# New prices and a looser dependency rule in the planner that writes a kernel's instruction order

## The chip, the cores and the metric

The kernel runs on one core of a Trainium2 chip. The metric is the device time of one execution in microseconds, the median over several runs. The core has five engines that work side by side, each with its own instruction queue that it goes through strictly in order: TensorE (PE in the profile, with its weight loads as PEld), VectorE (DVE), ScalarE (ACT), GpSimd (POOL) and SyncE (SP), which here only issues the transfers between memory and the core's SBUF. An instruction that needs another engine's result waits on a semaphore, and everything behind it on its engine waits with it.

## The reference

One inference step of a decoder with two layers and a width of 1024, for a prompt of 512 tokens and eight sample tokens that share all weights. In outline:

```python
h = x
for l in range(2):
    xn = rmsnorm(h, pre_norm_g[l])
    if l == 0:   # HGRN2: gated linear recurrence, 16 heads of 128
        q, fpre, i, z = split(xn @ w_in_a, 4)
        f = lb + (1 - lb) * sigmoid(fpre); k = 1 - f
        o, S = hgrn2_chunked(silu(q), log(f), k, i, S0)   # S_t = diag(f_t) S_{t-1} + k_t v_t^T
        mix = (rmsnorm(o, onorm_a) * silu(z)) @ w_out_a
    else:        # sliding window of 128, 32 query heads on 4 key/value heads, sinks, partial rotary
        k, v = split(rmsnorm(h, kv_norm_g) @ w_kv, 2)
        q, z = split(xn @ w_in_b, 2)
        mix = (window_attention(rope(q), rope(k), v, sinks) * silu(z)) @ w_out_b
    h = h + rmsnorm(mix, post_norm_g[l])
    h = h + (p[l] @ w_pe[l]) * sigmoid(h @ w_pg[l])
```

It returns h for all tokens, the final states of the recurrence and the new rows of keys and values. All arrays are 32-bit floats.

## The kernel before

Activations lie transposed, features on the 128 partitions and the 520 tokens along the free axis. A weight matrix is worked through in tiles of 128 output features; a tile takes up to 8 steps over the input features, and a step is six matmuls of 260 columns, because each 32-bit operand is split into a high and a low part (high x high, low x high, high x low, for two halves of the tokens). The weights come in loads of 512 KB into one of three buffers (`wr`); ScalarE copies the high part into `wh`, VectorE or GpSimd takes the difference into `wl` (`halves`, lines 649 to 659). TensorE sums a tile in a PSUM pair `pj`, and ScalarE or VectorE empties it. Beside this main stream run the chains of small steps: in layer A one chain a head (`hgrn` and `sample_a`), in layer B one a unit of attention heads (`unit_attn`). These use the four PSUM banks `ph`. The tiles `xs` and `og` hold the split inputs of the matmuls, `sb` the states of the sample tokens, `b` the small work tiles, `acc` the sums of squares for a norm.

A turn of a tile (`turn`, line 922) is done through memory: VectorE transposes blocks into `tmp`, one transfer writes them to `td`, and four transfers read them back, each into 32 partitions of the turned tile `xr`. In layer B, `query` (line 1266) swaps halves through `qd` in the same manner, with two writes and two reads.

The kernel has no fixed order of instructions. Every instruction is first entered into a plan (`Plan.enter`, line 187) with its level (MAIN, SIDE or FIRST), the engines that may run it, a price, and the earlier instructions that it depends on. `Plan.issue` (line 233) then plays the program through on model clocks, one for each engine, and writes the instructions out in the order in which the model starts them. That order is the program: on the chip nothing is reordered. What decides in it:

- `price` (line 142) gives each instruction's busy time, and whether it holds the port that VectorE and GpSimd share.
- `after` (line 241) adds a hand-over: `SAME` when maker and user are on the same engine, `LAT` for another engine, 0.1 for a transfer. `ready` (line 247) is the latest of these over an instruction's dependencies.
- `choose` (line 261) takes, on each engine, the instructions that could start first. On TensorE those that came ready less than `HAND` = 0.3 us ago go behind the others; on the three engines in `SHY` so do, in layer A, those that read a transfer landed less than `SAFE` = 1.5 us ago. Then the level decides, then the place in the program.
- A transfer starts when one of the `lanes` is free; its bytes go through one common `pipe`, and it lands some time behind that (lines 320 to 325). Loads that depend on nothing are held back while the pipe's backlog is over `BACKLOG`.
- A tile name taken from a fixed number of buffers has a maker, its first user. Every other instruction that touches the tile depends on the maker, whether or not the two touch the same bytes. The chip itself waits only for what overlaps.

The first loads, a warm-up of TensorE and six tiles of the embedding (`embed`) open the program; the masks `lmask` are made beside it on GpSimd and VectorE. Where a layer ends, the sums of squares go through a matmul with `ones`, a power on GpSimd (`rsr`) and a transposition into `R`, and then `residual` (line 777) makes the new `xs` step by step on VectorE and ScalarE, for the first matmuls of `gates` (line 798) with the weights `w_pg`. Tiles of the embedding fill TensorE meanwhile.

All instructions are recorded by one line of `enter`, 192, so the profile tells them apart by their tiles.

Of the kernel before, what the change touches and what calls it, by code (L numbers as in the profile page):

```python
# [53 lines left out]

SAME = {"tensor": -0.3, "vector": 0.05, "scalar": 0.1, "gpsimd": 0.02}
LAT = {"tensor": 0.28, "vector": 0.2, "scalar": 0.25, "gpsimd": 0.17}
HAND = 0.3
SAFE = 1.5
SHY = ("tensor", "vector", "scalar")

BEGIN = {"tensor": 0.9, "vector": 0.8, "scalar": 2.0, "gpsimd": 0.7, "sync": 0.0}

IDLE, SLOW = 3.4, 6.8
LATE = 1.5

RUNS = ((64, 4.0), (128, 2.0), (256, 1.4), (512, 1.15))
BACKLOG, CALM = 1.5, 40.0
# [27 lines left out]
class Plan:  # L95
# [46 lines left out]
    def price(self, engine, op, aps, a, k):  # L142
# [3 lines left out]
        if engine == "sync":  # L146
            run = min(self.run(x) for x in aps)
            return aps[0].nbytes() / 3.3e5 * next((f for n, f in RUNS if run <= n), 1.0), False
        if engine == "tensor":
            n, m = int(np.prod(aps[0].shape[1:])), int(np.prod(aps[1].shape[1:]))  # L150
            if op == "transpose":
                return 0.109, False
            if aps[1].dtype == F32:
                return 2 * max(0.025, 0.109 * m / P, n / 1200 + 0.003), False
            if aps[1].dtype == F32R:
                return max(0.109, 0.000453 * n + 0.002), False
            return n / 2400 + 0.003, False
# [7 lines left out]
        if engine == "scalar":  # L165

            t = 0.06 + 0.00086 * size * (3.2 if a[0].ap[-1][0] == NB else 1) + part
            if "accum_out" in k:
                t += 0.26 if AF.Exp in a else 0.19
            return t, False  # L170
# [3 lines left out]
        if op == "copy_predicated":  # L174
            return 0.09 + 0.0011 * size, False
        if op == "tensor_reduce":
# [10 lines left out]
    def enter(self, on, name, a, k):  # L187
# [6 lines left out]
        if any(x.tensor.name.startswith("tw") for x in ins[1:]):  # L194
            op.late = LATE
        self.ops.append(op)
        for x in ins:
            t = x.tensor.name
# [4 lines left out]
            if kept and t not in self.left:  # L203
                tag, bufs = self.homes.get(t, (t, 1))
                if tag not in self.slots:
                    self.slots[tag] = Slots(tag, bufs)
                self.slots[tag].order.append(t)
                op.news.append((tag, t))
                self.maker[t] = op
            elif kept:  # L210
                op.deps.add(self.maker[t])
            if t not in op.tiles and kept:
                op.tiles.add(t)
                self.left[t] = self.left.get(t, 0) + 1
        for x in outs:
# [8 lines left out]
            self.writes.setdefault(t, []).append((r, op))  # L224
        op.deps.discard(op)
        op.load = op.dma and not op.deps
        for d in op.deps:
# [5 lines left out]
    def issue(self):  # L233
        clock = dict(BEGIN)
        wait = {e: [] for e in clock}
        homes = {t: tag for tag, s in self.slots.items() for t in s.order}
        given, pipe, lanes, low, port, slow = set(), 0.0, [0.0] * 8, 0, 0.0, 0.0
        best = dict.fromkeys(clock)
        stale = set(clock)

        def after(d, e):

            if d.dma:
                return d.end + 0.1
            return d.end + (SAME if d.engine == e else LAT)[d.engine]

        def ready(op, e):
            return max((after(d, e) for d in op.deps), default=0.0)

# [11 lines left out]
        def choose(e):  # L261
# [13 lines left out]
            safe = SAFE if t > CALM and low < self.second else 0.0  # L275
            fresh = lambda op: any(d.dma and d.end + safe > t for d in op.deps)
            able.sort(
# [25 lines left out]
        while todo:  # L303
# [16 lines left out]
            if op.dma:  # L320
                t = max(t, lanes[0])
                clock[e] = t + 0.45
                pipe = max(pipe, t + 1.4) + cost
                op.end = pipe + 1.6 + op.late
                lanes = lanes[1:] + [op.end]
# [1515 lines left out]
```

## Time and profile before

| what | value |
|---|---|
| median of 3 runs | 1069.0 us (1067.67 to 1069.65) |
| the profiled execution | 1068.61 us |
| span of the program in it | 1066.8 us |
| granted TensorE clock, mean | 0.999 |
| TensorE busy | 1057.2 us, 8828 matmuls |
| VectorE, ScalarE, GpSimd busy | 904.7, 681.8, 114.0 us |
| moved by transfers | 178.99 MB, mean 168 GB/s |

The span runs from the first instruction to the last end in one profiled execution; the execution's own time is 1.8 us longer, for what lies around the program. A row of the stretches gives, for 27 us, the busy time of each engine with its number of instructions, the granted clock, the busy share of the transfer engines and the GB/s. A row in order of time gives start, length, engine, operation, tiles and shapes, a count where several of a kind were merged, and in brackets how long the engine sat idle before it and for whom. Groups give busy time, the mean of one in ns, and the idle time before. Layer A ends and layer B begins at some 570 to 620 us, and layer B ends from about 1000 us.

### The profile page before, as it was taken

To read this page: it belongs to the slowest core of one execution; us is meant where nothing else is said; L and a number is where in the kernel's file an instruction comes from. 1 tells how busy PE (TensorE), PEld (TensorE's weight loads), DVE (VectorE), ACT (ScalarE), POOL (GpSimd) and SP (SyncE) were. 2 spreads that over 40 slices of the span, in tenths; PEclk is the share of its full clock that TensorE was granted. 3 is DMA by queue.
4 is the path that set the end of the run, shared out by engine and by line. 5 is a ranking of instruction groups with operands and counts; after the bars stand their busy time and mean duration, and the time that the engine had idled before them with its cause. 6 is when DMAs were issued, how large, how long until landed. Compare 5 with 4: busy or idle time off the path is not lost.

```text
span 1066.8 us, 23981 instructions
## 1 busy us (share of the span) xinstructions
PE 1057.2 (99%) x8828; PEld 1051.2 (99%) x8828; DVE 904.7 (85%) x1963; ACT 681.8 (64%) x1829; POOL 114.0 (11%) x198
## 2 busy tenths in 40 slices
PE   9999999999999999999999999999999999999998
PEld 8999999999999999999999999999999999999998
DVE  8899788875787958788889999699999998999894
ACT  7877676655767637776636565477667664675542
POOL 1111121101111112111111000000100000002000
PEclk9999999999999999999999999999999999999999
DMA  9556586665646646576663454544433545423432
GB/s 314 183 190 183 143 247 195 191 195 156 213 155 206 193 130 224 177 210 191 190 223 142 159 190 142 170 121 136 124 101 115 164 155 186 154 82 124 156 100 81
DMA packets 147069, 178.99 MB, mean 168 GB/s; under 512 B 76932, under 2 KB 99660, under 8 KB 146952
## 3 DMA queue, kind: packets, MB, share of 16 engines
q1 hardware_dynamic: 146952, 177.46, 52.7%
q8 instruction: 70, 1.15, 0.4%
q14 instruction: 47, 0.39, 0.1%
HBM read 137.04 MB, written 34.86 MB: 161 GB/s over the span
## 4 chain that ended last, share of the span: by engine, by line
PE 91%; ACT 4%; DVE 3%; issue 1%; DMA 0%; POOL 0%; DVEq 0%; POOLq 0%
PE pj L192 71%; PE ph L192 21%; ACT g L192 1%; ACT wh L192 1%; DVE wl L192 1%; DVE x L192 0%; DMA wr<-in_w_pg 0%; ACT tmp L192 0%; ACT sb L192 0%; ACT b L192 0%; DVE acc L192 0%; ACT og L192 0%; DVE xr L192 0%; DVE tmp L192 0%; DVE g L192 0%
## 5 line engine op out<-in xcount | busy, mean ns | idle before, releaser
L192 PE MATMUL pj<-xs,wh 128*128 128x260 f32 (+2 forms) x3264 | 554.7, 285 | 1.6 <-ACT xs L192 1.3
L192 PEld LDWEIGHTS pj<-xs,wh 128*128 128x128 f32 x3264 | 457.7, 189 | 3.2 <-ACT xs L192 2.3
L192 PE MATMUL pj<-xs,wl 128*128 128x260 f32 (+2 forms) x1632 | 340.5, 285 | 0.0
L192 PEld LDWEIGHTS pj<-xs,wl 128*128 128x128 f32 x1632 | 255.1, 188 | 0.2
L192 ACT CAST wh<-wr 128x512 fp32r<-128x512 f32 x287 | 176.2, 619 | 111.1 <-PE pj L192 100.5
L192 DVE TENSOR_TENSOR wl<-wr,wh 128x512 fp32r<-128x512 f32 x275 | 187.6, 685 | 48.6 <-ACT wh L192 47.4
L192 PE MATMUL pj<-og,wh 128*128 128x260 f32 x1056 | 182.4, 285 | 0.3 <-ACT og L192 0.3
L192 PEld LDWEIGHTS pj<-og,wh 128*128 128x128 f32 x1056 | 149.5, 188 | 0.9 <-ACT og L192 0.5
L192 PE MATMUL pj<-og,wl 128*128 128x260 f32 x512 | 106.3, 284 | 0.1
L192 PEld LDWEIGHTS pj<-og,wl 128*128 128x128 f32 x512 | 79.9, 188 | 0.3 <-DVE wl L192 0.3
L192 ACT ACTIVATE sb<-sb,g 128x128 f32<-128x128 f32 x128 | 64.7, 556 | 2.4 <-DVE sb L192 2.4
L192 ACT ACTIVATE sb<-sb,nv 128x128 f32<-128x128 f32 x128 | 63.1, 555 | 0.3
L192 ACT COPY b<-ph 128x256 f32<-128x256 f32 (+1 forms) x80 | 27.8, 350 | 47.0 <-PE ph L192 46.5
L192 ACT ACTIVATE b<-b,an 128x129 f32<-128x129 f32 x128 | 50.6, 398 | 4.5 <-DVE an L192 4.4
L192 ACT ACTIVATE tmp<-pj 128x520 f32<-128x520 f32 (+2 forms) x48 | 24.5, 527 | 43.3 <-PE pj L192 43.2
L192 PE MATMUL ph<-xs,b 128*128 128x256 f32 (+1 forms) x360 | 50.5, 283 | 0.0
L192 DVE COPY_PREDICATED xr<-lmask,ph 128x256 f32<-128x256 int32 x96 | 46.8, 487 | 3.8 <-PE ph L192 3.4
L192 PE MATMUL ph<-xr,b 128*128 128x128 f32 x320 | 49.0, 275 | 0.3 <-ACT b L192 0.3
L192 DVE TENSOR_TENSOR x<-x,pj 128x520 f32<-128x520 f32 (+2 forms) x64 | 39.5, 621 | 10.8 <-PE pj L192 10.2
L192 DVE TENSOR_TENSOR g<-g,b 128x256 f32<-128x256 f32 x96 | 40.5, 422 | 9.3 <-ACT b L192 6.1
L192 DVE TENSOR_TENSOR xr<-xr,b 128x256 f32<-128x256 f32 x96 | 41.0, 427 | 8.6 <-PE ph L192 6.4
L192 PEld LDWEIGHTS ph<-xs,b 128*128 128x128 f32 x360 | 46.3, 188 | 0.1
(222 smaller groups left out, 1737.8 us busy)
## 6 DMA issues: line engine op xcount, KB each, us to landing
wr<-in_w_in_a SPq DMA_DIRECT2D x64, 512.0 KB, 4.5
sb<-sd SPq DMA_DIRECT2D x32, 512.0 KB, 4.5
wr<-in_w_in_b SPq DMA_DIRECT2D x32, 512.0 KB, 4.0
td<-tmp SPq DMA_DIRECT2D x45, 256.0 KB, 3.2
xr<-td SPq DMA_DIRECT2D x180, 64.0 KB, 3.2
sb<-in_state SPq DMA_DIRECT2D x16, 512.0 KB, 5.4
out_st_s<-sb SPq DMA_DIRECT2D x16, 512.0 KB, 3.0
wr<-in_w_out_a SPq DMA_DIRECT2D x16, 512.0 KB, 4.8
```

What stands on the lines that cost most here:

```text
L192: op = Op(len(self.ops), self.level, on, [lambda c=c: c(*a, **k) for c in calls], [self.price(e, name, ins, a, k) for e in on], on[0] == " ...
```

## The change

Four things change, all of them in the planner:

1. The hand-overs `SAME` and `LAT` get other values, most of them lower.
2. The model of transfers: SyncE's clock begins at 0.45 us; 16 transfers may be under way instead of 8; a transfer enters the pipe 1.2 us after its issue instead of 1.4 and lands 1.8 us (`LAND`) behind its bytes instead of 1.6; the rates are given outright, by the shortest contiguous run, and are lower for short runs.
3. The prices of instructions: on ScalarE by whether the input is in PSUM, with a term for a stride of eight elements and one for each operand that holds one value a partition (in place of the one for sums); on VectorE for predicated copies and for transposes; on TensorE in the last digits.
4. The dependency on a tile's maker is kept for the order (the maker is still issued first) but is left out of `ready` and of the question whether a transfer is fresh, unless the two overlap in the data.

```diff
-SAME = {"tensor": -0.3, "vector": 0.05, "scalar": 0.1, "gpsimd": 0.02}
-LAT = {"tensor": 0.28, "vector": 0.2, "scalar": 0.25, "gpsimd": 0.17}
+SAME = {"tensor": -0.28, "vector": 0.034, "scalar": 0.06, "gpsimd": 0.02}
+LAT = {"tensor": 0.31, "vector": 0.12, "scalar": 0.14, "gpsimd": 0.12}
 HAND = 0.3
+LAND = 1.8
-BEGIN = {"tensor": 0.9, "vector": 0.8, "scalar": 2.0, "gpsimd": 0.7, "sync": 0.0}
+BEGIN = {"tensor": 0.9, "vector": 0.8, "scalar": 2.0, "gpsimd": 0.7, "sync": 0.45}
-RUNS = ((64, 4.0), (128, 2.0), (256, 1.4), (512, 1.15))
+RATES = ((64, 5.0e4), (128, 1.0e5), (256, 1.4e5), (512, 2.3e5), (1e9, 3.0e5))
...
             run = min(self.run(x) for x in aps)
-            return aps[0].nbytes() / 3.3e5 * next((f for n, f in RUNS if run <= n), 1.0), False
+            return aps[0].nbytes() / next(r for n, r in RATES if run <= n), False
...
             if op == "transpose":
-                return 0.109, False
+                return 0.111, False
             if aps[1].dtype == F32:
-                return 2 * max(0.025, 0.109 * m / P, n / 1200 + 0.003), False
+                return 2 * max(0.025, 0.111 * m / P, n / 1200 + 0.003), False
             if aps[1].dtype == F32R:
-                return max(0.109, 0.000453 * n + 0.002), False
+                return max(0.111, 0.0004427 * n + 0.00475), False
...
         if engine == "scalar":
-            t = 0.06 + 0.00086 * size * (3.2 if a[0].ap[-1][0] == NB else 1) + part
-            if "accum_out" in k:
-                t += 0.26 if AF.Exp in a else 0.19
+            t = (0.06 if aps[1].space == PSUM else 0.085) + 0.00085 * size + part
+            if a[0].ap[-1][0] == NB and size > 64:
+                t += 0.0012 * size
+            near = sum(int(np.prod(x.shape[1:])) == 1 < size for x in aps[2:])
+            t += (0.1 if size > 64 else 0.15) * near
             return t, False
...
         if op == "copy_predicated":
-            return 0.09 + 0.0011 * size, False
+            return (0.07 + 0.00104 * size if apart else 0.1 + 0.00115 * size), False
+        if op in ("transpose", "stream_shuffle"):
+            return 0.1 + 0.00104 * size, False
...
+        makers = set()
         for x in ins:
...
             elif kept:
-                op.deps.add(self.maker[t])
+                makers.add(self.maker[t])
...
         op.deps.discard(op)
+        op.soft = makers - op.deps - {op}
+        op.deps |= op.soft
         op.load = op.dma and not op.deps
...
-        given, pipe, lanes, low, port, slow = set(), 0.0, [0.0] * 8, 0, 0.0, 0.0
+        given, pipe, lanes, low, port, slow = set(), 0.0, [0.0] * 16, 0, 0.0, 0.0
...
         def ready(op, e):
-            return max((after(d, e) for d in op.deps), default=0.0)
+            return max((after(d, e) for d in op.deps if d not in op.soft), default=0.0)
...
-            fresh = lambda op: any(d.dma and d.end + safe > t for d in op.deps)
+            fresh = lambda op: any(d.dma and d.end + safe > t for d in op.deps if d not in op.soft)
...
-                pipe = max(pipe, t + 1.4) + cost
-                op.end = pipe + 1.6 + op.late
+                pipe = max(pipe, t + 1.2) + cost
+                op.end = pipe + LAND + op.late
```

The computation, the tiles, the buffers and the number of instructions are the same; only their order, and which of VectorE and GpSimd takes a step that both may take, can differ.

## The prediction

> **What bounds the kernel now.** I read the page first, then the busy time by stretches, then what TensorE (PE) waited for, then the order of time around each of its waits. The page says that TensorE is the bound:
>
> ```profile
> span 1066.8 us, 23981 instructions
> PE 1057.2 (99%) x8828; PEld 1051.2 (99%) x8828; DVE 904.7 (85%) x1963; ACT 681.8 (64%) x1829; POOL 114.0 (11%) x198
> ```
>
> The change removes no matmul, so what it can win is TensorE's idle time, and that sits in few places. Stretches of 27 us, columns as in the page (busy PE first); left out are stretches that read 27.00, and one of them is shown:
>
> ```profile
> 0.00:27.00 27.00, 24.89 (x189) 23.09 (x190) 23.86 (x59) 19.44 (x38) 4.54 (x18) 1.00 0.90 313
> 27.00:54.00 27.00, 26.89 (x224) 26.66 (x224) 23.13 (x42) 22.93 (x47) 4.90 (x10) 1.00 0.54 179
> 54.00:81.00 27.00, 26.68 (x224) 26.44 (x223) 25.59 (x50) 20.13 (x48) 3.32 (x8) 1.00 0.59 199
> 81.00:108.00 27.00, 26.79 (x229) 26.59 (x229) 24.68 (x61) 20.62 (x57) 3.40 (x8) 1.00 0.62 185
> 135.00:162.00 27.00, 27.00 (x231) 27.00 (x230) 24.09 (x59) 19.79 (x49) 5.68 (x10) 1.00 0.83 259
> 567.00:594.00 27.00, 25.56 (x205) 24.50 (x204) 26.26 (x66) 17.36 (x44) 3.19 (x3) 1.00 0.54 186
> 594.00:621.00 27.00, 26.91 (x225) 26.71 (x224) 26.97 (x70) 17.94 (x49) 0.00 (x0) 1.00 0.43 153
> 675.00:702.00 27.00, 26.80 (x224) 26.54 (x224) 18.84 (x38) 17.29 (x50) 1.18 (x1) 1.00 0.46 142
> 999.00:1026.00 27.00, 25.87 (x215) 25.37 (x214) 26.32 (x69) 18.11 (x43) 2.53 (x2) 1.00 0.33 115
> 1053.00:1080.00 27.00, 9.78 (x81) 9.57 (x79) 3.37 (x9) 1.46 (x4) 0.00 (x0) 0.94 0.07 25
> ```
>
> Idle are 2.11 us in the first stretch, 0.11 + 0.32 + 0.21 to 108 us, 1.44 + 0.09 where layer A ends, 0.20 at 675, 1.13 where layer B ends, and 13.8 - 9.78 = 4.02 in the last. The last is the tail behind the final matmul (an activation, two VectorE steps, a store), which no order shortens. What TensorE waited for, with total, times and longest:
>
> ```profile
> PE pj L192 <- ACT xs L192: 1.3, 2, 0.8
> PE ph L192 <- DVE far L192: 1.1, 1, 1.1
> PE pj L192 <- DVE g L192: 0.9, 2, 0.6
> PE ph L192 <- ACT b L192: 0.5, 2, 0.3
> PE ph L192 <- DVE acc L192: 0.5, 1, 0.5
> PE ph L192 <- POOL rsr L192: 0.4, 1, 0.4
> PE pj L192 <- ACT og L192: 0.3, 1, 0.3
> PE ph L192 <- DVE ad L192: 0.2, 1, 0.2
> ```
>
> The 1.1 us on far is the launch. The other ten waits make 4.1 us. An idle gap shows less than it costs, because matmuls overlap:
>
> ```profile
> 652.55 33.96 PE pj L192 x283
> L192 PE MATMUL pj<-xs,wh 128*128 128x260 f32 x2944 | 496.7, 285 | 0.1
> ```
>
> One matmul each 33.96 / 283 = 0.120 us, while one lasts 0.285: a gap hides 0.285 - 0.120 = 0.165 us before it is seen. After a gap a pair takes 0.48 us (the matmul row at 5.24 us, below) where 0.285 + 0.120 = 0.405 is usual: 0.08 more. I take 0.25 us on top of each gap. Ten waits cost 4.1 + 2.5 = 6.6 us. The gaps too short for the list (about 4.5 us of idle inside, less 4.1) add 0.4, and with some five of them another 1.3. So 8.3 us is the ceiling of any better order.
>
> **The change part by part.** All of it acts through the order that the planner writes; no engine works faster.
>
> *Prices of TensorE.* A 260-column matmul goes from 0.000453 x 260 + 0.002 = 0.1198 to 0.0004427 x 260 + 0.00475 = 0.1199 us, beside the measured 0.120. Cost nothing; a wrong price here would move every stretch, and it is right in both.
>
> *The first loads (a loss).* SyncE now begins at 0.45 instead of 0, and a load lands at 1.2 + size / 3.0e5 + 1.8. The first 128 KB piece was planned for 1.4 + 0.40 + 1.6 = 3.4 us and is now planned for 0.45 + 1.2 + 0.44 + 1.8 = 3.9. The trace has it earlier than both:
>
> ```profile
> 2.92 0.41 ACT L192 CAST wh<-tmp 128x256 fp32r<-128x256 f32 x1 [0.60 <-DMA tmp<-in_w_pe]
> 2.99 1.33 DVE L192 TENSOR_SCALAR lmask<-lmask 128x256 int32<-128x256 int32 x4 [0.32 <-POOL lmask L192]
> 5.24 0.48 PE L192 MATMUL pj<-g,wh 128*128 128x260 f32 x2 [0.63 <-DVE g L192]
> ```
>
> Mask steps, which nothing needs yet, already fill VectorE ahead of what TensorE waits for, and a later planned landing invites one more (1.33 / 4 = 0.33 us). Bounds 0 and 0.5 (the shift); I take +0.3, nearest to one mask step.
>
> *Prices of ScalarE (a gain).* At 57.34 TensorE waits for a copy that ScalarE reached late:
>
> ```profile
> 55.41 0.54 ACT L192 ACTIVATE sb<-sb,g 128x128 f32<-128x128 f32 x1
> 55.84 0.71 ACT L192 ACTIVATE g<-g,ones 128x512 f32<-128x512 f32 x1
> 56.46 0.54 ACT L192 ACTIVATE sb<-sb,g 128x128 f32<-128x128 f32 x1
> 56.90 0.39 ACT L192 COPY b<-g 128x256 f32<-128x256 f32 x1
> 57.34 0.71 PE L192 MATMUL ph<-xr,b 128*128 128x128 f32 x4 [0.32 <-ACT b L192]
> ```
>
> From start to start the first three take 56.90 - 55.41 = 1.49 us. Old prices: 0.06 + 0.00086 x 128 x 3.2 = 0.41, 0.06 + 0.00086 x 512 = 0.50, 0.41, in all 1.32: 0.17 short. New: 0.085 + 0.109 + 0.154 + 0.1 = 0.45, 0.085 + 0.435 + 0.1 = 0.62, 0.45, in all 1.52: right. The two waits on ACT b cost 0.5 + 2 x 0.25 = 1.0, and the idle of 27 to 54 us, 0.11, with its 0.25 makes 0.4. Bounds: 0 (the copy has other reasons to be late) and 1.4. The prices are off just there, so I take -1.2. The wait on ACT og I leave as it is, since no row says what would fill it.
>
> *End of layer A, 567 to 594 us.* The idle 1.44 + 0.09 with some six gaps of 0.25 is 3.0 us.
>
> ```profile
> 572.75 0.41 DVE L192 TENSOR_TENSOR acc<-acc,tmp 128x256 f32<-128x256 f32 x1
> 573.45 1.46 POOL L192 TENSOR_TENSOR wl<-wr,wh 128x512 fp32r<-128x512 f32 x1 [17.61 <-ACT wh L192]
> 573.69 1.85 DVE L192 TENSOR_TENSOR acc<-acc,tmp 128x256 f32<-128x256 f32 x2
> 575.25 0.60 PE L192 MATMUL ph<-ones,acc 128*128 128x1 f32 x4 [0.50 <-DVE acc L192]
> 587.75 5.01 DMA wr<-in_w_pg
> 592.79 1.14 ACT L192 CAST b<-wr 128x512 fp32r<-128x512 f32 x2 [1.22 <-DMA wr<-in_w_pg]
> ```
>
> Three causes: first, two VectorE additions took 1.85 us while GpSimd worked, where one just before took 0.41; TensorE lost 0.50 + 0.25 = 0.75. Second, ScalarE sat 1.22 us before a weight piece whose load took 5.01 us; the casts of xs that TensorE wants stand behind it. The old price of that load is 1.4 + 1.59 + 1.6 + 0.1 = 4.69, the new 1.2 + 1.75 + 1.8 + 0.1 = 4.85: half of the 0.32 us that was missing. Third, VectorE is full (26.26 and 26.97 of 27 us), which no price changes. Bounds 0 and -2.25 (3.0 less the 0.75); I take -1.0, nearer to 0 because of the full VectorE.
>
> The Trainium skill, page SBUF — State Buffer, section SBUF: two separate sides, says that VectorE with two SBUF inputs and GpSimd take one shared pair of ports as an exclusive lock, and that the loser waits for the whole instruction. The 1.85 us beside the 1.46 agree. By that rule it is decided by which starts first on the chip, and the 0.75 us stay or fall by chance, and the sum is as it stands; were it a matter of prices alone, the sum would end 0.75 lower.
>
> *End of layer B and 675 us.* The idle 1.13 with two gaps of 0.25 is 1.63 us, and at 675 it is 0.20 + 0.25 = 0.45. The first has the same chain of norm and casts on a VectorE that is busy 26.32 of 27. Bounds 0 and -2.1; I take -0.7, a third, as above.
>
> *A tile's first user.* This acts on transfers above all. Four reads fill one turned tile; the later three were planned behind the landing of the first, though their rows are apart:
>
> ```profile
> xr<-td SPq DMA_DIRECT2D x180, 64.0 KB, 3.2
> 313.64 0.57 SPq L192 DMA_DIRECT2D xr<-td  x1
> 316.42 1.93 SPq L192 DMA_DIRECT2D xr<-td  x3
> ```
>
> The gap of 2.8 us is the planned landing. Now the four go out together and the tile is whole about 2 us sooner, 45 times. It wins nothing: between 108 and 567 us, where most of them are, TensorE reads 27.00, and before that no wait in the list is on a transfer. The short pieces of these reads are priced higher too (64 KB in runs of 128 bytes from 0.40 to 0.66 us), which holds weight loads back in the plan by up to 4 x 0.26 = 1.0 us a turn; sixteen transfers may be in flight instead of eight, which lets them go earlier. The cover of it all: a weight load behind three such issues leaves 1.9 us later (the row above), and three weight buffers last 3 x 48 x 0.120 = 17 us. If that cover were gone, each turn would cost up to 1.9 + 1.0 us.
>
> *VectorE's prices.* A predicated copy of 256 from PSUM goes from 0.37 to 0.34 us, a transpose gets 0.03 more. Cost nothing: a shift this small is under the 0.3 us by which TensorE waits a fresh step out. Without that it would be 0.03 a step.
>
> *Hand-overs.* ScalarE's falls from 0.25 to 0.14 us and VectorE's from 0.20 to 0.12. The copy at 56.90 ends at 57.29 and TensorE starts at 57.34: price and hand-over were 0.28 + 0.25 = 0.53, are 0.30 + 0.14 = 0.44, and measure 0.44. So 0.09 us of slack goes from each. Bounds 0 and +8.8 (the rival below); I take +0.0 because TensorE still ranks a step that came ready under 0.3 us ago behind all others.
>
> Sum: +0.3 - 1.2 - 1.0 - 0.7 = -2.6 us. The profiled execution took 1068.6 us, and 1066.0 follows; the median of the three runs is 0.4 higher, and on it I forecast **1066.4 us**. What a measurement can tell from no change is about 0.2%, 2.1 us.
>
> **The rivals.**
>
> *The waits only move (no change).* VectorE at 26.26, 26.97 and 26.32 of 27 us is the true limit at both ends of layers; then only the ScalarE term is won: -1.2 + 0.3 = -0.9, 1068.1 us. For it: these three rows. Against it: 5.01 us of a load planned at 4.69 is a fault of price.
>
> *The slack was needed (slower).* TensorE takes its steps in a fixed order, so one late hand-over stops all behind it.
>
> ```profile
> L192 ACT COPY b<-g 128x256 f32<-128x256 f32 x80 | 32.0, 401 | 8.8 <-DVE g L192 7.5 <-PE ph L192 1.0
> ```
>
> These 80 copies, and about 50 others of their kind in layer A, feed TensorE, and 2 of them stop it now. With 0.09 us less, a late one costs about 0.09 + 0.25 = 0.34. Above (2.6 + 2.1) / 0.34 = 14 late ones the kernel is slower; one in seven, 18, gives 6.1 - 2.6 = +3.5, 1072.5 us. Bound: one in five, 26, is 8.8 - 2.6 = +6.2. Against it stands the 27.00 of the stretches from 108 to 567 us, where even ScalarE prices that were short by 0.17 stopped nothing.
>
> *The rule of the first user does nothing.* If the chip itself held the later three reads until the first had landed, the new order would have SyncE wait there. SyncE would lose 2.8 us a turn, and the turned tiles would come no sooner; with the other terms as they are, 1066.4 again. The same time, so it shares the forecast's chance.
>
> **How the numbers follow.** Forecast 0.44, waits that only move 0.31, slack needed 0.25. Each case spreads: the forecast from two thirds of the 8.3 us ceiling (-5.5, 1063.5) to the edge at 1066.9, the second to 1071.1, the third from there up. The range 1063.5 to 1073.0 leaves one in ten at each side; the likeliest case alone is 1063.5 to 1066.9. Faster 0.44, same 0.31, slower 0.25.
>
> **What would show it.** Right: TensorE's busy time stays at 1057 and its idle inside falls from 4.5 us to about 3; no wait on ACT b before 108 us; the wait of ScalarE on the weight load at the end of layer A under 0.8 us; the first matmul on real data at 5.2 to 5.7 us; the four reads of a turn issued together. Wrong: new waits on copies (ACT b, ACT g) in stretches that read 27.00 now, which is the slower case; or the same idle at 567 and 999 us with VectorE still above 26, which is no change. Any idle stretch of several us where none was would make it wrong in a way that I do not foresee: a new order that leaves a buffer late.

## The result and the profile after

The changed kernel takes 1073.4 us (median of 5 runs, 1073.2 to 1074.7), the kernel before beside it 1068.5 (1067.7 to 1069.7). The ratio is 1.0050, with an interval of 1.0036 to 1.0063: slower by 4.9 us, where I had forecast 2.6 us less. The profiled execution took 1074.71 us, its span is 6.1 us longer than that of before. The page after:

```profile
span 1072.9 us, 23983 instructions
PE 1060.2 (99%) x8828; PEld 1053.7 (98%) x8828; DVE 906.2 (84%) x1968; ACT 680.8 (63%) x1829; POOL 116.4 (11%) x193
```

The matmuls are as many as before; 3.0 us of the 6.1 are in TensorE's busy time, which also grows when matmuls run slowly, and 3.1 in its idle time. The stretches after, columns as before:

```profile
0.00:27.00 27.00, 23.83 (x163) 21.93 (x164) 22.80 (x55) 18.93 (x37) 4.41 (x17) 1.00 0.91 308
135.00:162.00 27.00, 26.69 (x226) 26.49 (x225) 22.57 (x51) 17.73 (x48) 4.74 (x11) 1.00 0.49 143
567.00:594.00 27.00, 26.61 (x223) 26.28 (x222) 26.23 (x65) 18.83 (x45) 1.66 (x2) 1.00 0.53 166
675.00:702.00 27.00, 26.16 (x217) 25.77 (x216) 20.23 (x37) 17.92 (x57) 1.43 (x1) 1.00 0.45 140
702.00:729.00 27.00, 26.12 (x216) 25.67 (x215) 25.20 (x50) 16.78 (x48) 2.38 (x3) 1.00 0.38 112
783.00:810.00 27.00, 25.99 (x213) 25.37 (x213) 25.93 (x62) 17.17 (x63) 2.72 (x2) 1.00 0.37 101
999.00:1026.00 27.00, 25.89 (x216) 25.42 (x215) 25.50 (x63) 17.27 (x42) 2.26 (x2) 1.00 0.46 155
```

567 to 594 us is better by a whole microsecond, from 54 to 108 us, not shown, the idle time is gone. But 702 to 729 and 783 to 810 us, which read 27.00 before, have lost 0.9 and 1.0, 675 to 702 has 0.84 idle instead of 0.20, and the first stretch 3.17 instead of 2.11. What TensorE waited for after:

```profile
PE ph L197 <- DVE b L197: 1.7, 2, 0.9
PE pj L197 <- DVE g L197: 1.2, 1, 1.2
PE ph L197 <- DVE far L197: 1.1, 1, 1.1
PE ph L197 <- DVE g L197: 1.0, 1, 1.0
PE pj L197 <- ACT xs L197: 0.8, 2, 0.4
PE pj L197 <- DVE wl L197: 0.8, 1, 0.8
PE ph L197 <- POOL rsr L197: 0.7, 1, 0.7
PE ph L197 <- DVE xr L197: 0.3, 1, 0.3
```

The waits on ACT b, ACT og and DVE acc are gone. VectorE has taken their place, with few and long stops. To see where time was lost, busy or idle, I gave every matmul its usual pitch (0.120 us for 260 columns, 0.118 for 256, and so on; the sum is the same in every kernel here) and worked out from the matmuls' starts how much later than the kernel before each kernel had done the same work. I call this its lag. Single entries are good to some 0.4 us: so far do they move with another choice of the usual pitches.

```
where before is at  after  l_ties  l_table  l_four  s_a30  n_b071   (us later)
10                  2.31    0.87    2.10     0.12    0.89   0.46
30                  2.96    1.50    2.70     0.91    1.49   1.00
100                 1.77    0.27    1.55    -0.27   -0.50   0.49
160                 2.57    0.62    2.35     0.08   -0.18   0.71
520                 2.94    1.00    2.73     1.33    0.00   1.05
640                 0.93   -0.98    0.44    -0.99   -2.12   4.13
700                 1.76   -0.17    0.14    -0.83   -1.00   3.79
730                 3.11    0.13    1.43    -0.58    0.59   4.91
820                 5.19    1.34    3.61     0.28    1.18   4.68
1000                5.60    1.60    3.90     1.07    3.74   4.09
last matmul's end   5.49    1.45    3.85     1.00    3.69   4.11
behind it           0.61    0.61    0.61     0.37    0.01   0.00
```

The other columns belong to the experiments. After loses 3.0 us in the first 30, wins 1.2 up to 100, loses 0.8 near 145, wins 2.0 at the end of layer A, loses 4.3 between 640 and 820 and 0.6 behind the last matmul. Four things in the trace stand at the places of loss.

*The start.*

```profile
1.78 0.89 DVE L192 TENSOR_SCALAR lmask<-lmask 128x256 int32<-128x256 int32 x2 [0.77 <-POOL lmask L192]
2.24 3.01 DVE L197 TENSOR_SCALAR lmask<-lmask 128x256 int32<-128x256 int32 x9 [1.22 <-POOL lmask L197]
5.17 0.41 DVE L197 TENSOR_TENSOR wl<-tmp,wh 128x256 fp32r<-128x256 f32 x1
6.07 0.77 PE L197 MATMUL pj<-g,wh 128*128 128x260 f32 x2 [1.20 <-DVE g L197]
6.64 0.64 PE L197 MATMUL pj<-g,wl 128*128 128x260 f32 x2
```

The first row is of the kernel before, which had these two and the four at 2.99 us: nine mask steps instead of six stand ahead of the first difference of weights. TensorE begins on data at 6.07 instead of 5.24 us, and then two matmuls take 0.64 us where 0.40 is usual, a pitch of 0.215 instead of 0.120, until about 10 us. I call this half pitch. Of the five executions three took 1073.2 to 1073.4 us and two 1074.7, the profiled one among these; so the half pitch, some 1.5 us of the 3.0, is probably not in the median.

*VectorE beside GpSimd.* At two places a VectorE step takes over a microsecond more than its like, and TensorE stops behind it:

```profile
700.57 1.68 POOL L197 TENSOR_TENSOR g<-g,tmask 128x512 fp32r<-128x512 f32 x1 [43.77 <-DVE g L197]
701.00 1.79 DVE L197 SCALAR_TENSOR_TENSOR g<-tmp,g 128x512 fp32r<-128x512 f32 x1
708.35 0.30 PE L197 MATMUL ph<-ident,b 128*128 128x128 f32 x1 [0.87 <-DVE b L197]
806.05 0.16 DVE L197 TENSOR_TENSOR og<-bg,og 128x8 fp32r<-128x8 f32 x1
806.55 1.43 POOL L197 TENSOR_TENSOR wl<-wr,wh 128x512 fp32r<-128x512 f32 x1 [5.47 <-DMA qd<-g]
806.73 1.28 DVE L197 TENSOR_TENSOR og<-bg,og 128x8 fp32r<-128x8 f32 x1
809.34 0.50 PE L197 MATMUL ph<-g,x 128*128 128x512 f32 x1 [1.01 <-DVE g L197]
```

The planner keeps the two apart on its model clocks only; nothing in the program makes GpSimd wait for VectorE there.

*The table of ScalarE.*

```profile
690.18 1.28 ACT L197 ACT_TABLE_LOAD   x1
691.47 0.40 ACT L197 ACTIVATE b<-b,an 128x129 f32<-128x129 f32 x1
694.66 0.30 PE L197 MATMUL ph<-ident,b 128*128 128x128 f32 x1 [0.84 <-DVE b L197]
```

The first Exp of layer B loads its table for 1.28 us, which no price holds. In the kernel before the same load began at 692.48 us, and the only stop behind it was the 0.20 us at 698.

*The end.* Before, the last two sums ran one behind the other; after, they alternate:

```profile
1067.87 0.29 PE L197 MATMUL ph<-xs,b 128*128 128x264 f32 x1
1067.99 0.28 PE L197 MATMUL pj<-xs,b 128*128 128x264 f32 x1
1068.61 0.78 DVE L197 SCALAR_TENSOR_TENSOR tmp<-tmp,g 128x264 f32<-128x264 f32 x2 [4.24 <-ACT tmp L197]
1069.31 0.77 DVE L197 TENSOR_TENSOR og<-og,tmp 128x264 f32<-128x264 f32 x2
```

Both end together, so VectorE has two steps of each kind behind the last matmul instead of one: 4.67 us to the span's end, where it was 4.06.

### The profile page after: what moved, and what is told of

It reads as the page before. It is cut to its first block, busy times and chain, and to the rows that moved or that the text cites. A ratio compares the mean times of both kernels' runs of the same rounds, so it can differ in the third digit from the quotient of the medians.

```text
span 1072.9 us, 23983 instructions
## 1 busy us (share of the span) xinstructions
PE 1060.2 (99%) x8828; PEld 1053.7 (98%) x8828; DVE 906.2 (84%) x1968; ACT 680.8 (63%) x1829; POOL 116.4 (11%) x193
## 3 DMA queue, kind: packets, MB, share of 16 engines
q8 instruction: 70, 1.15, 0.4%
## 4 chain that ended last, share of the span: by engine, by line
PE 90%; DVE 5%; ACT 2%; issue 1%; POOL 1%; DMA 0%; POOLq 0%; DVEq 0%; ACTq 0%
PE pj L197 71%; PE ph L197 19%; DVE tmp L197 1%; DVE g L197 1%; DVE wl L197 1%; ACT b L197 0%; DVE og L197 0%; ACT g L197 0%; ACT wh L197 0%; DVE acc L197 0%; POOL lmask L197 0%; DVE ao L197 0%; ACT sb L197 0%; DMA wr<-in_w_in_b 0%; DVE b L197 0%
## 5 line engine op out<-in xcount | busy, mean ns | idle before, releaser
L197 PE MATMUL pj<-xs,wh 128*128 128x260 f32 (+2 forms) x3264 | 593.0, 290 | 0.9 <-ACT xs L197 0.8
L197 PEld LDWEIGHTS pj<-xs,wh 128*128 128x128 f32 x3264 | 472.8, 189 | 2.2 <-ACT xs L197 1.5
L197 PE MATMUL pj<-xs,wl 128*128 128x260 f32 (+2 forms) x1632 | 354.7, 290 | 0.0
L197 PE MATMUL pj<-og,wh 128*128 128x260 f32 x1056 | 189.1, 287 | 0.1
L197 PE MATMUL ph<-xs,b 128*128 128x256 f32 (+1 forms) x360 | 62.1, 283 | 0.0
L197 PE MATMUL ph<-xr,g 128*128 128x256 f32 (+1 forms) x256 | 60.6, 275 | 0.0
L197 PE MATMUL ph<-xr,b 128*128 128x128 f32 x320 | 58.9, 275 | 0.3 <-DVE xr L197 0.3
L197 POOL TENSOR_TENSOR wl<-wr,wh 128x512 fp32r<-128x512 f32 x18 | 23.6, 1312 | 318.4 <-ACT wh L197 202.5
L197 ACT COPY b<-g 128x256 f32<-128x256 f32 (+1 forms) x112 | 41.0, 376 | 16.6 <-DVE g L197 13.1
L197 PEld LDWEIGHTS ph<-xr,b 128*128 128x128 f32 x320 | 49.5, 190 | 0.8 <-DVE xr L197 0.5
```

The costliest lines, as they stand in the source:

```text
L197: op = Op(len(self.ops), self.level, on, [lambda c=c: c(*a, **k) for c in calls], [self.price(e, name, ins, a, k) for e in on], on[0] == " ...
```

## Experiments

Theory: the loss is these places, each with a cause of its own. Rival: the slack was needed, that is, the thinner hand-overs. Medians stand with the ratio to the kernel before (1068.0 to 1068.5 in each group) and its interval.

**Local edits behind the plan.** The order of the changed kernel is kept, and single instructions are moved or added. `done` is the list of instructions in the planned order:

```diff
+ # l_masks: the lmask steps of VectorE go behind 27.5 us of the plan
+ at = next(n for n, x in enumerate(rest) if x[2] == "vector" and x[0] > 27.5)
+ done[:] = rest[:at] + mine + rest[at:]
+ # l_ties: a 128x1 product of what VectorE wrote last, ahead of three GpSimd steps
+ calls.insert(0, lambda y=y: nc.gpsimd.tensor_tensor(tie, y, y, op=ALU.mult))
+ # l_table: an Exp of one column at 620 us of the plan
+ done[at][5].insert(0, lambda: nc.scalar.activation(early, one, AF.Exp))
```

> The changed kernel with its order kept, only that the 12 mask steps of VectorE (lmask) are taken out of the first microseconds and put behind the steps of the stage at 27 us. Theory of the three causes: the nine mask steps ahead of the cast of the first weights and of the first g cost TensorE its start (first data matmul at 6.07 us instead of 5.24, then matmuls at half pitch to about 9.9 us), so the first data matmul comes before 5.2 us, the wait on wl at 18 us stays or shrinks, and the time falls by 1.5 to 2.9 us, to 1070.5 to 1072. The other stops (694, 701, 708, 809 us) stay as they are. Rival, the slack of the hand-overs: the start is worth 0.8 us at the most (the difference of the first idle), 1072.6 or above, and waits on copies appear.

> The changed kernel with its order kept, only that GpSimd gets three small multiplies of 128x1 that read what VectorE has just written, so that its products at 145, 701 and 807 us begin behind the VectorE step that they collided with. Theory of the three causes: the VectorE steps of 1.79 us (g at 701 us) and 1.28 us (og at 807 us) go back to 0.7 and 0.2 us, TensorE's stops at 145, 708 and 809 us (0.31, 0.87 and 1.01 us) go or fall under 0.3 us, and the time falls by 2.0 to 2.8 us, to 1070.6 to 1071.4. Rival, the slack of the hand-overs: the stops are late hand-overs that any step would give, they only move, and the time stays within 0.7 us of 1073.4. If the products now collide with the next VectorE step instead, steps above 1 us show at other places and the test says nothing on the rival.

> The changed kernel with its order kept, only that ScalarE does one more activation of one column with Exp near 620 us, where it has time, so that its table is there before the first Exp of layer B. Theory of the three causes: the load of 1.28 us at 690 us moves to about 620 us, the stop on b at 694.66 us (0.84 us) goes, and the time falls by 0.8 to 1.1 us, to 1072.3 to 1072.6. Rival: the stop at 694 us has another cause (VectorE is late by itself), it stays, and the time is that of the changed kernel, 1073.4 within 0.4.

> The changed kernel with its order kept and the three edits together: mask steps behind 27 us, three ties on GpSimd, the Exp table loaded near 620 us. Theory of the three causes: the parts add up, -1.5 to -2.9, -2.0 to -2.8 and -0.8 to -1.1, so 1066.6 to 1069.1, at or below the kernel before (1068.5). Rival, the slack of the hand-overs: the thinner slack is still there and the time stays above 1071.5, with stops at new places.

Measured: l_masks 1074.45 (1.0055, 1.0043 to 1.0067), l_ties 1071.45 (1.0033, 1.0021 to 1.0045), l_table 1073.1 (1.0045, 1.0031 to 1.006), l_three 1070.38 (1.0019, 1.001 to 1.0027).

The ties do what the theory said: none of the three VectorE steps is longer than its like, and the stops at 145, 708 and 809 us are gone; the median is at the upper edge of the forecast. The step at 701 us in l_ties, with GpSimd behind its tie:

```profile
699.07 0.68 DVE L197 SCALAR_TENSOR_TENSOR g<-tmp,g 128x512 fp32r<-128x512 f32 x1
701.42 0.20 POOL L385 TENSOR_TENSOR tie<-g 128x1 f32<-128x1 f32 x1 [46.52 <-DVE g L197]
```

In l_table the stop at 694 us is gone and the lag grows by 1.1 us less from 640 to 700; the median fell by only 0.3, less than expected. l_masks missed: the first matmul on data comes at 4.53 us, but the gain is lost at 31 us, where eleven of the mask steps that I had moved there held up the norm:

```profile
27.03 2.68 DVE L197 TENSOR_SCALAR lmask<-lmask 128x256 int32<-128x256 int32 x11
29.63 0.15 DVE L197 TENSOR_SCALAR rsm<-ph 128x3 f32<-128x3 f32 x1
...
30.77 0.32 PE L197 MATMUL ph<-ident,rsr 128*128 128x128 f32 x1 [1.59 <-POOL rsr L197]
```

l_three, with that fault in it, is 3.0 us faster than the changed kernel, and with the thin hand-overs untouched: against the rival, though above the 1069.1 of the theory.

**One part of the change alone, on the kernel before.** The four parts are those listed under the change.

```diff
  p_hand:        SAME and LAT as after
  p_transfers:   BEGIN, LAND, RATES, 16 lanes, 1.2 as after
  p_first_user:  op.soft as after
  p_prices:      price() as after, but for the transfers
```

> The kernel before with one part of the change alone: the hand-overs of ScalarE and VectorE, 0.25 to 0.14 us and 0.20 to 0.12 us. Rival, the slack of the hand-overs: this part alone carries the loss, the time goes up by 2 to 6 us, to 1070.5 to 1074.5, with new waits of TensorE on copies (ACT b, ACT g). Theory of the three causes: the hand-overs are right and cost nothing; the new order differs, and what its time is depends on which VectorE and GpSimd steps happen to meet and on the first microseconds: within 1066.5 to 1071, and any loss is found as stops that begin with VectorE steps above 1 us beside GpSimd.

> The kernel before with one part alone: the model of the transfers (start, size and run length, sixteen in flight, SyncE's begin). Theory of the three causes: the later planned landing of the first piece lets mask steps in ahead of the first cast, so the first data matmul comes later than 5.24 us; beside that its own order. The planned order has pauses of TensorE in layer A, since short pieces are dearer there and a turned tile's reads still wait one on another in the plan; if the chip keeps these pauses in the order, it is slower by 1 to 4 us, 1069.5 to 1072.5. Rival, the slack of the hand-overs: this part is harmless, 1067.5 to 1069.5.

> The kernel before with one part alone: the rule of a tile's first user. My prediction priced it at nothing: 1068.5 within 1 us. Theory of the three causes: the rule itself costs nothing, but it makes a new order with new meetings of VectorE and GpSimd: 1066.5 to 1071. Rival: the rule lets transfers start so early that a weight load comes late: new waits of TensorE on DMA or on casts of weights (ACT xs, DVE wl), above 1070.

> The kernel before with one part alone: the prices of ScalarE, VectorE, GpSimd and TensorE. My prediction: the two waits on ACT b before 108 us go, -1.2 us from that. Theory of the three causes: they go, and the rest of the order is as good or bad as its meetings of VectorE and GpSimd: 1066 to 1071. Rival, the slack of the hand-overs: with the old hand-overs there is slack enough, so this one is at most 1068.5.

Measured: p_hand 1077.1 (1.0082, 1.0066 to 1.0098), p_transfers 1089.04 (1.0192, 1.0174 to 1.0209), p_first_user 1072.81 (1.0037, 1.0026 to 1.0048), p_prices 1077.88 (1.009, 1.0073 to 1.0107). All four are above what the theory gave. The rival's range holds p_first_user alone, but TensorE has no wait on a transfer there, and its waits on ACT xs sum to the 1.3 us of before. The four losses sum to 44 us, nine times the loss of all parts together. So the parts have no times that add. The stops are of every kind and at new places; p_transfers has them where a turned tile or its weights come late:

```profile
PE ph L193 <- DVE b L193: 3.9, 4, 2.8
PE ph L193 <- DVE xr L193: 3.2, 5, 1.5
PE pj L193 <- ACT wh L193: 3.1, 3, 1.4
```

In p_hand the largest are on rsr (2.6 us) and xs (1.4); on ACT b it is one of 0.5. So its time goes the rival's way, and beyond its 1074.5, but its waits don't.

**One number of TensorE.** I had overlooked that `SAME` of TensorE goes from -0.30 to -0.28. The next matmul of a sum comes ready at the last one's end plus `SAME`, and `choose` puts it behind the others if that plus `HAND` = 0.30 lies in the future: 0.00 does not, 0.02 does. That is why TensorE alternates.

```diff
  s_a30 (after):  -SAME = {"tensor": -0.28, ...   +SAME = {"tensor": -0.30, ...
  s_b28 (before): -SAME = {"tensor": -0.30, ...   +SAME = {"tensor": -0.28, ...
  s_h30 (p_hand): -SAME = {"tensor": -0.28, ...   +SAME = {"tensor": -0.30, ...
```

> The changed kernel with one number back: SAME of TensorE -0.30 instead of -0.28. Theory of the threshold: the next matmul of a sum comes ready at the end of the last one plus SAME, and choose() puts it behind all others if that is under HAND = 0.3 us ago; -0.30 + 0.30 is not above 0, -0.28 + 0.30 is. So in the changed kernel TensorE leaves every sum after one matmul and alternates between two, and with -0.30 it stays on one again. Then the last two sums end one behind the other instead of together, the stretch behind the last matmul falls from 4.67 to 4.06 us, the middle has an order of its own again, and the time falls by 0.6 us at the least, to 1070.5 to 1072.8; steps of VectorE above 1 us beside GpSimd stay possible at new places. Rival, the slack of the hand-overs (those of VectorE and ScalarE are as thin as in the changed kernel): 1073 or above, with waits on copies.

> The kernel before with one number of the change: SAME of TensorE -0.28 instead of -0.30. Theory of the threshold: TensorE alternates, the stretch behind the last matmul grows from 4.06 to 4.67 us, and most of the loss of the changed kernel is here: 1069.5 to 1075. Rival, the slack of the hand-overs: a hand-over longer by 0.02 us between matmuls gives more slack, not less, and costs nothing: 1067.7 to 1068.7. Rival, the order as such: any new order costs what its meetings and late hand-overs cost; then the time is up while the stretch behind the last matmul explains 0.6 us of it only and the stops of TensorE explain the rest.

> The kernel before with the hand-overs of the change, except that SAME of TensorE stays at -0.30. With it at -0.28 the time was 1077.1. Theory of the threshold: the loss of that kernel came from the alternating TensorE; with -0.30 the time is 1066 to 1070, and the end behind the last matmul is 4.06 us. Rival, the slack of the hand-overs: the thin hand-overs of VectorE and ScalarE carry the loss, the time stays above 1073, with waits of TensorE on copies (ACT b, ACT g) of 0.1 to 0.5 us in many places.

Measured: s_a30 1072.65 (1.0035, 1.002 to 1.005), s_b28 1078.55 (1.0083, 1.0057 to 1.0109), s_h30 1079.14 (1.0087, 1.006 to 1.0113). The mechanism at the end is shown: with -0.30 the last two sums are whole again, here in s_a30, and what lies behind them is 4.07 us; with -0.28 in the kernel before it is 4.66.

```profile
1060.47 3.08 PE L197 MATMUL ph<-xs,b 128*128 128x264 f32 x24
1063.38 3.09 PE L197 MATMUL pj<-xs,b 128*128 128x264 f32 x24
```

But as the reason for the whole loss the theory falls: s_h30 was to take 1066 to 1070, and s_b28 is above the 1075 it was given. The number is worth the 0.6 us at the end; beyond that it makes one more order. The rival has s_h30's time on its side, above 1073, and two waits on copies, 0.7 us on ACT b and 0.6 on ACT g, not many small ones. Such waits come with the old hand-overs too: 1.4 us on ACT g and 0.3 on ACT b in s_b28, 1.3 on ACT b in n_b069 below. So they don't tell thin hand-overs from a new order.

**An edit that means nothing.** The price of VectorE's steps in the kernel before, 1 ns up or down.

```diff
-        t = 0.07 + 0.00104 * size + part
+        t = 0.071 + 0.00104 * size + part    # n_b071; n_b069: 0.069
```

> The kernel before with the base price of a VectorE step at 0.071 instead of 0.070 us, an edit that says nothing true or false of the chip. The order as such: the planner writes another order, and its time differs from 1068.2 by some 2 to 6 us, most likely upward, through stops at places that the price has nothing to do with; then a few us of any change here are the luck of an order. If the time stays within 0.7 us of 1068.2, orders are all about equally good, and the loss of the changed kernel is from its edits.

> The kernel before with the base price of a VectorE step at 0.069 instead of 0.070 us. If the order as such sets a few us, this is another order with another time, 1069 to 1076, and the kernel before is at the good end of its neighbours. If the other nudge was one bad order, this one is within 1 us of 1068.3, or faster.

Measured: n_b071 1072.87 (1.0035, 1.002 to 1.005), n_b069 1071.09 (1.0019, 1.0009 to 1.003). So 1 ns costs 4.4 and 2.9 us. In n_b071 nearly all is lost at one place:

```profile
536.26 0.38 PE L192 MATMUL ph<-tmp,ones_r 128*128 128x256 f32 x1 [0.39 <-ACT tmp L192]
537.39 0.38 PE L192 MATMUL ph<-tmp,ones_r 128*128 128x256 f32 x1 [0.30 <-DVE tmp L192]
538.96 0.51 PE L192 MATMUL pj<-og,wh 128*128 128x260 f32 x2 [1.18 <-ACT wh L192]
541.68 0.64 PE L192 MATMUL pj<-og,wh 128*128 128x260 f32 x2
```

Ten other orders of the same work were timed: the changed one, seven from its parts, two from 1 ns. All lie between 1071 and 1089 us, none at or below the 1068.3 of before. The kernel before is at the good end of its neighbours.

**Do the named places account for the loss?** l_pauses moves nine mask steps into the first 13 us, behind the casts that TensorE waits for. l_four has these, the ties, the table, and the last two sums sorted. b_four makes the first three edits on the kernel before, with one tie at 569 us of the plan, b_tie the tie alone, and a_again is the changed kernel once more.

```diff
+ # l_pauses, l_four, b_four: nine lmask steps at 5 to 13 us of the plan
+ while later and x[2] == "vector" and x[0] > later[0][0]:
+     rest.append(later.pop(0)[1])
+ # l_four: the last 48 matmuls, first all of one sum, then of the other
+ last.sort(key=lambda x: x[3].outs[0].tensor.name != first)
```

> The changed kernel with its order kept; of the twelve mask steps of VectorE nine are moved behind the first casts and sums, one or two at a time, all within the first 13 us. Theory of the start: the first data matmul comes before 5.2 us, no half pitch follows, there is no stop on rsr near 31 us, and the time falls by 1.5 to 2.9 us, to 1070.5 to 1072. Rival: TensorE that starts sooner waits for the weights that come next (wh and wl at 14 to 16 us, 1.5 us in the kernel with masks behind 27 us), so the gain is given back there and the time stays at 1072.5 or above.

> The changed kernel with its order kept and all local edits: masks as in the kernel beside it, the three ties on GpSimd, the Exp table loaded near 620 us, and the last 48 matmuls sorted so that their two sums end one behind the other and not together. Theory of the causes: 1070.4 was measured with three edits and a stop of 1.6 us on rsr; without that stop and with an end shorter by 0.6 us it is 1067.8 to 1069.2, no slower than the kernel before. Rival: something not named is left, 1070 or above.

> The kernel before with its own order kept and the same kinds of edit: nine mask steps behind the first casts, one tie on GpSimd at 569 us (where two VectorE additions took 1.85 us), the Exp table near 620 us. If the causes are faults that both orders have, and not faults of the change, this gains too: start 0.3 to 0.8, stop on acc at 575 us 0.5 to 0.75, stop at 698 us 0.2 to 0.4, so 1066.4 to 1067.5. Rival: what is gained at the start is waited for at the next weights, and a stop removed at 575 us comes back at 582 to 591 us: 1068 to 1069.

> The changed kernel, unchanged, timed once more. Theory of the start: the first data matmul is at 6.07 us as in every kernel with this beginning, and half pitch follows in some executions and not in others, so the times fall into two groups 1.3 us apart, near 1073.3 and 1074.7. If the profile of this run has the full pitch, its span is 1.3 us shorter than 1072.9. Rival: the half pitch belongs to this order, then it is there again and the times do not split.

> The kernel before with one edit: a 128x1 multiply on GpSimd that makes its difference of weights at 573 us begin behind the VectorE addition that it collided with. Theory of the meetings: the two additions of 1.85 us go back to 0.8, the stop on acc at 575 us goes, and as in b_four the order gains 0.8 to 1.1 us there, so 1067.1 to 1067.6 if nothing gives it back. Rival: VectorE is full there and the next stop (582 to 591 us) takes the gain: 1068.0 to 1068.6.

Measured: l_pauses 1073.36 (1.0048, 1.0032 to 1.0065), l_four 1068.72 (1.0002, 0.9993 to 1.0012), b_four 1069.38 (1.0012, 1.0001 to 1.0023), a_again 1073.53 (1.005, 1.0038 to 1.0063), b_tie 1068.6 (1.0007, 0.9997 to 1.0016).

l_four is the main result: with the order of the change kept and its four places mended, nothing is left of the loss that the runs can tell from noise. Its largest waits beside the launch:

```profile
PE pj L197 <- ACT xs L197: 0.8, 2, 0.4
PE pj L197 <- DVE wl L197: 0.7, 1, 0.7
PE ph L197 <- POOL rsr L197: 0.7, 1, 0.7
PE ph L197 <- DVE xr L197: 0.7, 1, 0.7
PE pj L197 <- ACT wh L197: 0.4, 1, 0.4
```

No copy is among them, with the hand-overs as thin as in the change. The single edits do not add up to it, though: 0.0 for l_pauses, 2.0 and 0.3 for ties and table, and 0.24 us that the end is shorter (4.43 instead of 4.67) make 2.5 of the 4.7 us. Place by place the lag agrees better: against the changed kernel, l_four is 2.0 us ahead at 30 us, gains 3.0 between 640 and 820 and 0.24 behind the last matmul, and gives 0.9 back between 160 and 520. But half pitch at the start is part of the 2.0. Part of the gap in the medians may be chance in the start, too: a_again took 1073.3 to 1073.9 four times and 1075.05 once, and that execution, the profiled one, had the half pitch. l_pauses lags 0.7 us at 30 us and not 3.0, but its four runs, 1072.3 to 1074.2, do not show it, and its median is in the rival's range; what the masks cost in the median stays open.

On the kernel before, b_four is slower than theory and rival had it: it gains 1.2 us at the end of layer A and loses 0.9 of it at 630 us, where TensorE waited 0.65 us for rsr; my own table load had run on ScalarE 3 us earlier, and b_tie, without it, has no such stop. In b_tie the two additions go back from 1.85 to 0.77 us and the stop at 575 us goes; the lag falls by 1.15 us there. Its profiled execution had already lost 1.06 by 20 us, at waits for first weights, and the median is that of before. No kernel here beats the kernel before.

## Why the prediction was wrong

**The step that failed** is the form of the sum. It took the stops of the old order, asked which would go, and let every stretch that read 27.00 stay so. But the change writes the whole order anew, and a new order has stops of its own: there was no term for them. In the changed kernel the lag grows by 4.3 us between 640 and 820 us, most of it in stretches that read 27.00 before. Two edits of 1 ns put such a term at 2.9 and 4.4 us, above the 2.6 that I summed up. I had named "any idle stretch of several us where none was" as what I would not foresee, without a price.

**First loads, +0.3.** Too small. The mechanism was right, more mask steps in front, but three came in and not one, and the half pitch behind it was not in the sum. In the profile 3.0 us are lost by 30 us, and 1.5, still three times my bound of 0.5, in kernels with the same beginning and full pitch (l_ties, s_a30). The first matmul came at 6.07 us, not at 5.2 to 5.7.

**ScalarE's prices, -1.2.** Right as to the waits: those on ACT b are gone, and p_prices, which has the new prices alone, has TensorE busy for all 81 us from 27 to 108. The size is not shown to come from them: the lag falls by 1.2 us from 30 to 100 us in the changed kernel, but by about 0.1 in p_prices, and by about 1.5 in p_first_user, which has the old prices.

**End of layer A, -1.0.** Right in sign, more than I took: 2.0, near the bound of 2.25. ScalarE's wait of 1.22 us for a weight load is gone, and so is the meeting at 573 us, which I had left to chance. But that the new price of the load did it is not shown, and the sign may be luck: in n_b069, with the old price and the old rules, both are gone as well, and the lag falls by 1.9 us there. Its stretch, 25.56 in the kernel before:

```profile
567.00:594.00 27.00, 26.48 (x217) 25.81 (x217) 26.90 (x68) 18.15 (x45) 1.81 (x2) 1.00 0.56 191
```

The chance of a meeting then struck at 145, 701 and 807 us: the 0.75 us of one meeting I had seen, and not asked how many the new order would have. The Trainium skill, page SBUF — State Buffer, section SBUF: two separate sides, has the loser of the shared ports wait for the whole instruction; an addition of eight columns that took 1.28 us beside a product of 1.43 agrees.

**End of layer B and 675 us, -0.7.** Nothing was won at 999 us (25.89 of 27), and at 694 the stop grew from 0.20 to 0.84 behind a table load that I had not looked for in the trace of before.

**First user 0, TensorE's prices 0, hand-overs 0.** The sign that I gave for the first user's rule came: from the first to the fourth read of a turn the median falls from 3.8 to 2.0 us, in the changed kernel and in p_first_user. By itself it shows no wait on a transfer, as I had it, but p_first_user is 4.6 us slower as an order. In the hand-overs I argued that TensorE "still ranks a step that came ready under 0.3 us ago behind all others" and did not put the new -0.28 into that rule: 0.6 us at the end, in the tail that "no order shortens". It can be lengthened.

**The rivals.** "The slack was needed" gave 1072.5, close to the time, by a mechanism that did not happen in the changed kernel: no wait on ACT b or ACT g, and l_four keeps the order of the thin hand-overs at 1068.7. "The waits only move" failed with the forecast: it had no new stops either.

## What to carry to other kernels

Where a planner writes the order, a better price is not a better order: first time a few edits that mean nothing, and weigh any forecast against their scatter. Where an order is at the good end of that scatter, as the one before was of eleven, even a better model is likely to lose at first. Two steps that a plan keeps apart only on model clocks can meet wherever two engines drift, unless the program ties them, and a cost that no price holds, like a table load, falls wherever the order puts it. Mending such places took the loss away here, but made no kernel faster than the one before.

## What the runs showed of the hardware

A stop can cost much more than its idle time. In n_b071 three stops within 3 us, 1.87 us together, were followed by half pitch to about 542.8 us, and the clock row says so:

```profile
536.02:539.43 3.41, 1.69 (x10) 1.30 (x10) 2.94 (x8) 1.74 (x4) 1.01 (x1) 1.00 0.88 308
539.00:543.00 4.00, 3.84 (x18) 3.57 (x19) 4.00 (x9) 1.56 (x3) 0.00 (x0) 0.57 0.78 278
```

The trace's record of the granted clock has it at half from 539.44 to 542.85 us. A single stop of 2.12 us in p_hand was not followed by it. The Trainium skill, page TensorE: Matmul & The Clock Gate, section What's actually happening, explains the clock by how busy TensorE was in windows of about 3.4 us that run free of the program. The lengths agree: the half clock in n_b071 lasts 3.413 us, as do one in s_b28 and two in p_transfers, and the full clock ahead of it, 532.48 us, is 156 times as long. But how busy TensorE was in one window does not settle it here. The 3.41 us ahead of n_b071's half clock, above, have it busy for 1.69 us; the window of p_hand with its long stop, counted in such steps from where its clock record begins, has it busy for less and was not followed by half clock:

```profile
587.19:590.60 3.41, 1.51 (x13) 1.51 (x14) 1.14 (x3) 0.68 (x2) 1.85 (x1) 1.00 0.51 154
```

The half pitch at the start of the changed kernel is of the clock too, though the granted clock reads 1.00 there, and only the 18 matmuls in 4 us show it:

```profile
6.00:10.00 4.00, 3.93 (x18) 3.96 (x19) 2.65 (x8) 1.24 (x2) 0.00 (x0) 1.00 1.03 323
```

The trace's clock records begin, at full clock, only at 10.05 us, where the half pitch ends, and the row counts what has no record as full. In a_again they begin at 10.41 us. In l_ties, with the same instructions up to the first matmuls on data, they begin at 5.23, ahead of these matmuls, which have full pitch; in the kernel before at 4.23. So the half pitch of the start lasted until the clock was first granted in full, and with the same instructions that came ahead of the data in one execution and behind it in another.
